# Attention projections as fill of a delta rule's stage: query, key and value products in pieces of two token tiles

## The chip, the core and the metric

The kernel runs on one core of a Trainium2 chip. Five engines work side by side, each on its own list of instructions in the order in which the program gives them: TensorE (PE) multiplies matrices, VectorE (DVE) and ScalarE (ACT) work on rows of SBUF and PSUM, GpSimd (POOL) on SBUF, and SyncE (SP) issues most transfers between the core's memory and the main memory (DMA); ScalarE issues the weights' transfers of the middle stage. Products land in PSUM and are taken out by VectorE or ScalarE. The metric is the time of one execution in microseconds (us); several executions give a median.

## What is computed

One layer of a hybrid block over 1,024 latent tokens and 256 context tokens, 1,024 channels, all in fp32. Cut to what matters:

```python
h  = rms_norm(x) * (1 + scale) + shift           # hc: the same for ctx
qkv_a, z_a, a_raw, b_raw, q_b, k_b, v_b, z_b, gates = split_cols(h @ w_in)
...
# branch A: 8 heads; q, k, v after a short convolution and SiLU, q and k normed
for d in range(2):                               # both directions
    s_ctx, _ = gdn_chunk_scan(ctx, state=0)      # chunked gated delta rule
    _, ol = gdn_chunk_scan(latent, state=s_ctx)  # o_t = S_t^T q_t
    o_lat = o_lat + ol
# branch B: differential softmax attention, 8 heads of 2 x 64
q_l = axial_rope(rms_norm(q_b, q_norm_w))
k_l = axial_rope(rms_norm(k_b, k_norm_w));  k_c = rms_norm(k_bc, k_norm_w)
o_b = (softmax(q1 k1) - lam * softmax(q2 k2)) @ v_b
merged = sig(g_a) * ((norm(o_a) * silu(z_a)) @ w_oa) + sig(g_b) * ((norm(o_b) * silu(z_b)) @ w_ob)
x = x + gate * (merged @ w_out)
```

## The kernel before

A product of fp32 precision is made of three products in the fast format: every operand is split into a high part (`hi`, a cast on ScalarE) and the rest (`lo`, a subtraction on GpSimd or VectorE), and hi x hi, hi x lo and lo x hi are summed in PSUM. So one tile of a projection is 8 x 3 = 24 products. A unit of weights is 256 columns of `w_in` in the first stages and 128 in the middle one.

The stages, as `run` (from L670) builds them:

1. The front (`front`, L239): modulation and norm of x, transposed into the tiles `hs`; among its end the first value unit, which brings the raw gates of the delta rule as well (`v_unit(0)`).
2. Eight units of queries and keys (`qk_unit`, `qk_finish`, from L591) and one of values. A unit makes ten tiles (keys) or eight (queries) of 128 tokens by 256 columns on TensorE (L456). When all are there, `qk_finish` works on the whole unit at once: square and norm, the rotation with tables (`qk_tables`), 128x128 transposes (L642), a split into two parts (L646, L647), one store for each four token tiles (L648).
3. The delta rule's projections with their convolution: one query unit (`emit_q_first`), eight of keys and values (`emit_kv`). Then the third value unit.
4. The delta rule's stage. Here the order of all engines is written by hand: streams (generators) offer one operation each with the engine, a duration, and what it waits for; `flow` (L86) takes the operation that could start first by its own clock, with a bias for each stream, and `step` emits it. The order so found is fixed in the program; each engine keeps to it on the chip. `PEL` (L55) is an amount that the planner adds before a TensorE product uses a result of another engine. The streams:
   - `preps(0)` and `preps(1)`: the preparation of heads (`gdn_prep`, L1016), two in turn. It computes the decay (ScalarE), key products `gram` and query-key products `qk` (masked on GpSimd in `masked`), stores blocks through the memory tensor `da` into `ab`, solves 31 rows of a triangular system by 62 small VectorE operations (L1089, L1091, "substitution"), brings the result back through `db`, merges blocks (`pz`, `p2`, `p3`, `pz6`, `pu6`) and stores `xd` and `qkd`.
   - `scan(0)` and `scan(1)`: the two directions' recurrences, ten chunks for each head, with products `chain` (from L1231); `out_chunk` for the outputs. Both directions of one head run side by side, the heads one after the other.
   - `loads`, `sets`, `tails`: what a scan reads, and the gated, transposed result of a head (`oT`).
   - The fill, which TensorE takes when nothing else is ready: the last value unit (`v_flow`), then 38 units of 128 columns (`fill_flow`): six query units of the delta rule (`query_out`, `query_conv`, with the convolution on VectorE) and 32 units for the gates z_a, z_b and the merge gates (`gate_out`). Their weights come by `weights`. The stage ends when the last head's tail is done; what is left of the fill is taken in the attention's opening by `rest`.
5. The attention (`attention`, a written table of due times) with the first half of the merge (`branch_a`) beside it, and the end (`phase3`).

The scans' tiles (pool `g4`, opened by `gdn_more`) lie where the last value unit's tiles and the 256-column weights lay, so scans can only start when that unit is through. SP issues in order, and so does every engine.

## Time and profile before

| | us |
|---|---|
| median of 3 runs (2168.3 to 2170.21) | 2168.44 |
| the profiled execution | 2174.7 |
| its span, first to last instruction | 2172.9 |
| mean granted clock of TensorE | 0.969 |
| busy: TensorE, VectorE, ScalarE, GpSimd | 2051.0, 1480.2, 1003.2, 938.1 |

The profile is of one execution and gives each instruction's start and length. A line number is that of the program above; `L71` is the helper through which the middle and last stages record every matrix product, so these are told apart by the names of their tiles (`mm`: projections, `chain`: scans, `s`: attention). An fp32 product outside the fast format shows as two instructions. A TensorE instruction's length is longer than its distance from the next one, since they are pipelined; a price is better read from a stretch and its count. The granted clock is the share of full speed at which TensorE was allowed to run.

### The profile page before, as it was taken

How to read it: one execution, taken by the hardware profiler on the slowest of the kernel's cores; microseconds unless marked ns; L12 is line 12 of the kernel's file. 1: busy time of each engine (PE TensorE's matmuls, PEld its weight loads, DVE VectorE, ACT ScalarE, POOL GpSimd, SP SyncE). 2: the span in 40 equal slices, each digit the busy share in tenths (PEclk: the TensorE clock that was granted, in tenths of full speed). 3: DMA queues.
4: the chain of work that ended last, by engine and by line, in shares of the span. 5: the costliest groups of instructions: out<-in, count | busy, mean ns of one | idle time of the engine just before them, and what ended most of it. 6: DMA issues, size and time to landing. Idle time of an engine off the chain costs nothing. (4 is left out here: it accounts for less than half of the span.)

```text
span 2172.9 us, 37989 instructions
## 1 busy us (share of the span) xinstructions
PE 2051.0 (94%) x14207; PEld 1719.1 (79%) x14207; DVE 1480.2 (68%) x3412; ACT 1003.2 (46%) x2133; POOL 938.1 (43%) x669
## 2 busy tenths in 40 slices
PE   8999999999999898999899899999999999998999
PEld 4999998887798677777777688776777777777899
DVE  4867776877766879788658756126788888873532
ACT  4322222443444344536545364346777777763210
POOL 2265663043322345252342424324766666764122
PEclk9999999999899899999999899998999999998999
DMA  9323335666676454565754646738454564227442
GB/s 317 97 80 127 108 107 175 164 165 171 179 180 223 122 165 148 181 210 162 235 169 154 211 152 204 210 120 230 104 149 129 148 193 130 91 83 232 144 150 86
DMA packets 379850, 347.99 MB, mean 160 GB/s; under 512 B 143007, under 2 KB 320769, under 8 KB 378643
## 3 DMA queue, kind: packets, MB, share of 16 engines
q1 hardware_dynamic: 333411, 302.05, 46.6%
q10 hardware_dynamic: 46256, 43.52, 6.2%
q8 instruction: 112, 1.84, 0.4%
q14 instruction: 71, 0.58, 0.1%
HBM read 228.96 MB, written 116.55 MB: 159 GB/s over the span
## 5 line engine op out<-in xcount | busy, mean ns | idle before, releaser
L71 PE MATMUL mm<-hs,wh 128*128 128x512 f32 x1216 | 421.5, 418 | 2.0 <-ACT zo L910 1.8
L456 PE MATMUL mm<-wh,hs 128*128 128x256 f32 (+1 forms) x1632 | 304.2, 287 | 0.5 <-DVE abt L658 0.3
L1441 DVE TENSOR_SCALAR_CACHE_REDUCE S<-s 128x512 f32<-128x512 f32 (+1 forms) x384 | 223.3, 597 | 98.4 <-PE s L71 97.2
L71 PEld LDWEIGHTS mm<-hs,wh 128*128 128x128 f32 x1216 | 234.6, 196 | 44.7 <-ACT zo L910 2.4
L456 PEld LDWEIGHTS mm<-wh,hs 128*128 128x128 f32 x1632 | 257.2, 192 | 1.1 <-DVE abt L658 0.6
L71 PE MATMUL mm<-hs,wl 128*128 128x512 f32 x608 | 253.7, 417 | 0.8 <-POOL wl L836 0.8
L433 PE MATMUL mm<-hs,wh 128*128 128x512 f32 (+1 forms) x832 | 230.9, 365 | 13.9 <-ACT xc L473 13.9
L1471 POOL TENSOR_TENSOR S<-S 128x1280 f32<-128x1280 f32 x64 | 188.5, 2945 | 109.0 <-ACT S L1466 104.2
L456 PE MATMUL mm<-wl,hs 128*128 128x256 f32 (+1 forms) x816 | 232.5, 286 | 0.0
L836 POOL TENSOR_TENSOR wl<-wr,wh 128x512 fp32r<-128x512 f32 x74 | 105.2, 1442 | 241.1 <-ACT wh L835 170.3
L433 PEld LDWEIGHTS mm<-hs,wh 128*128 128x128 f32 x832 | 151.8, 195 | 39.9 <-ACT xc L473 16.5
L1452 ACT ACTIVATE S<-S,mn 128x1280 f32<-128x1280 f32 x128 | 175.0, 1367 | 18.0 <-DVE mn L1445 17.4
L456 PEld LDWEIGHTS mm<-wl,hs 128*128 128x128 f32 x816 | 156.9, 192 | 0.0
L433 PE MATMUL mm<-hs,wl 128*128 128x512 f32 (+1 forms) x416 | 150.9, 363 | 0.0
L1487 ACT CAST ah<-t 128x512 fp32r<-128x512 f32 (+1 forms) x192 | 98.2, 512 | 101.4 <-PE t L74 98.7
L71 PE MATMUL s<-kh,qs 128*128 128x512 f32 (+1 forms) x384 | 139.5, 403 | 2.6 <-DVE S L1441 2.4
L71 PEld LDWEIGHTS mm<-hs,wl 128*128 128x128 f32 x608 | 119.5, 197 | 22.3 <-POOL wl L836 1.3
L478 DVE SCALAR_TENSOR_TENSOR ac<-xc,smallT,ac 128x1284 f32<-128x1284 f32 (+1 forms) x72 | 122.8, 1705 | 10.5 <-ACT ac L474 8.6
L1089 DVE TENSOR_TENSOR tmp<-ab,ts 80x31 f32<-80x31 f32 (+15 forms) x248 | 116.6, 470 | 16.3 <-DMA ab<-da 10.4
L1091 DVE TENSOR_TENSOR ts<-ts,tmp 80x31 f32<-80x31 f32 (+15 forms) x248 | 121.7, 491 | 6.1
L1494 DVE TENSOR_TENSOR al<-t,ah 128x512 fp32r<-128x512 f32 (+1 forms) x192 | 113.6, 592 | 7.7 <-ACT ah L1487 7.3
L74 PE MATMUL t<-ct,S 128*128 128x128 f32 x640 | 103.4, 277 | 6.8 <-DVE al L1494 6.8
(312 smaller groups left out, 5053.8 us busy)
## 6 DMA issues: line engine op xcount, KB each, us to landing
wr<-in_w_in_dram SPq DMA_DIRECT2D x21, 1024.0 KB
wr<-in_w_in_dram ACTq DMA_DIRECT2D x37, 512.0 KB
X<-gcd SPq DMA_DIRECT2D x16, 640.0 KB
xd<-X SPq DMA_DIRECT2D x16, 640.0 KB
x<-xd SPq DMA_DIRECT2D x80, 128.0 KB
kh<-kd SPq DMA_DIRECT2D x32, 320.0 KB
wa<-in_w_ada_dram SPq DMA_DIRECT2D x8, 1024.0 KB
qd<-col SPq DMA_DIRECT2D x16, 512.0 KB
```

Of the source, the lines that this page charges most:

```text
L71: self.nc.tensor.matmul(out, lhsT, rhs, start=start, stop=stop)
L74: self.nc.tensor.transpose(out, src, self.ident[:src.shape[0], :src.shape[0]])
L433: nc.tensor.matmul(pt[:, :n], wt[:, k, cs], ht[:, k, o:o + n], start=i == 0, stop=i == 3 * KT - 1)
L456: nc.tensor.matmul(pt[:, j * W:j * W + n], ht[:, k, ts], wt[:, k, :n], start=i == 0, stop=i == 3 * KT - 1)
L478: nc.vector.scalar_tensor_tensor(ac[:, w], xc[:, o + j:o + j + wd // parts], self.convw(j, ct), ac[:, w], ALU.mult, ALU.add)
L836: t2 = yield POOL, 1.36, [t1], lambda: nc.gpsimd.tensor_tensor(lo[:, k], raw[:, k], hi[:, k].bitcast(F32), ALU.subtract)
L1089: t = yield DVE, n * w / 960.0 + 0.11, [t, t1], lambda: V.tensor_tensor(tv, ab[:, j + 1:, j:j + 1].to_broadcast([80, n, w]), ts[:, j, :w]. ...
L1091: t = yield DVE, n * w / 960.0 + 0.11, [t, t1], lambda: V.tensor_tensor(ts[:, j + 1:, :w], ts[:, j + 1:, :w], tv, ALU.subtract)
L1441: self.nc.vector.tensor_scalar(x[c][:, o:o + m], x["s", j, c][:, :m], 1.0, None, ALU.mult, ALU.min, accum_out=x["m3"][:, c, j:j + 1])
L1452: self.nc.scalar.activation(S, S, AF.Exp, bias=x["mn"][:, c:c + 1], scale=-1.0, accum_out=w["l0"][:, c, t:t + 1])
L1471: self.nc.gpsimd.tensor_tensor(x[0], x[0], x[1], ALU.add)
L1494: self.nc.vector.tensor_tensor(y["al", k][:, :, q], x["t", k][:, :nb * P].rearrange("p (j f) -> p j f", f=P), y["ah", k][:, :, q].bitcast( ...
```

## The change

The delta rule's projections come right after the first value unit: all four query units (`emit_q`), then as before keys and values between them, and one value unit. The attention's eight query and key units and two of three value units become "parts", the first fill of the delta rule's stage, in the order keys, values, queries. A part's tile is now finished by itself, two token tiles (128 x 512) at a time in two slots: three ScalarE operations take it out of PSUM (`part_out`), then norm, rotation, transposes, split and two stores of 128 KB or so follow (`part_post`). Then come 32 gate units as fill; the six query units and their convolution are no longer in the stage.

```diff
-PEL = 0.05
+PEL = 0.4
...
+    def load_w(self, src, ab=False):
...
         for s in range(2):
             k = slice(s * KT // 2, (s + 1) * KT // 2)
-            nc.scalar.copy(hi[:, k], raw[:, k])
+            raw = self.wr.tile([P, KT // 2, n], F32, tag="wr", name="wr")
+            nc.sync.dma_start(raw[:, :, :w], src.rearrange("(k p) n -> p k n", p=P)[:, k])
...
+            nc.scalar.copy(hi[:, k], raw)
...
-                        self.units(qk + vs[:1], kv[0])
+                kv = qu[:1] + [... keys and values as before ...] + qu[1:]
...
+                parts = [("k", p) for p in range(4)] + [("v", 2), ("v", 3)] + [("q", p) for p in range(4)]
...
+                    def fill():
+                        yield from self.part_flow(parts)
+                        self.zo = self.hc.tile([P, 2, L], F32, tag="s21", name="zo")
+                        yield from self.fill_flow(todo)
+
+                    def more():
+                        yield lambda: sum(self.posted) == sum((NL if k == "q" else NT) // 2 for k, _ in parts)
+                        cx.close()
+                        self.gdn_more(gr)
+                        yield lambda: False
...
-                        self.flow(lambda: self.tailed == H)
+                    self.flow(lambda: self.tailed == H and self.units_done >= len(todo) - self.LEFT)
...
+    def part_flow(self, parts):
...
+            for t0 in range(0, NL if kind == "q" else NT, 2):
+                yield lambda: len(free) > self.nb
+                pt = self.pm.tile([P, 512], F32, tag="mm", name="mm")
+                for j in range(2):
...
+                            t = yield PE, 0.1195, [free[self.nb], tw], lambda: self.mm(
+                                pt[:, j * W:j * W + W], ht[:, k, o:o + P], wt[:, k], m == 0, m == 3 * KT - 1)
...
+    def part_out(self, kind, pair, t0, pt, t, free, n):
+        nc, s, tk = self.nc, n % 2, self.tk
+        yield lambda: self.posted[s] >= n // 2
...
+        for hf in range(2):
+            tr = yield ACT, 0.35, [t, old], lambda: nc.scalar.copy(raw[:, hf]...., v[:, hf])
+        t = yield ACT, 0.478, [t, old], lambda: nc.scalar.activation(sq, pt, AF.Square)
...
+    def part_post(self, kind, pair, t0, raw, sq, tr, t, s):
...
+        t = yield DVE, 0.6, [t], lambda: V.tensor_reduce(ss, ...)
+        tw = yield DVE, 0.08, [t], lambda: V.tensor_scalar(ss, ss, 1.0 / 64, EPS, ALU.mult, ALU.add)
...
+            for hf in range(2):
+                t1 = yield POOL, 0.7, [t, tr, tt], lambda: Q.tensor_tensor(m[hf], x[1 - hf], T(1, 1 - hf), ALU.mult)
+                if hf == 0:
+                    tw = yield POOL, 1.65, [tw], lambda: self.power(ss, ss)
+                t2 = yield DVE, 0.35, [tr, tt], lambda: V.tensor_tensor(o[hf], x[hf], T(0, hf), ALU.mult)
+                te += [(yield DVE, 0.35, [t1, t2], lambda: V.tensor_tensor(o[hf], o[hf], m[hf], ...))]
...
+        te = yield POOL, 1.3, [te, tw], lambda: Q.tensor_tensor(f8, f8, ss..., ALU.mult)
...
+                t1 = yield PE, 0.109, [te, b], lambda: self.tr(...)
...
+        th = yield ACT, 0.478, [t1, self.slot_t[s]], lambda: nc.scalar.copy(col[0], pv)
+        tl = yield DVE, 0.6, [th, self.slot_t[s]], lambda: V.tensor_tensor(col[1], pv, col[0].bitcast(F32), ALU.subtract)
...
-        self.asides[0].append(self.masked(h, qk, tQ))
+        self.kT_t, self.gram = [tX[1][-1], tQ], h + 1
...
+                    if n == "qk":
+                        u["tqk"] = yield POOL, 0.72, [u["tqk"]], lambda: nc.gpsimd.tensor_tensor(
+                            x, x, (self.up, self.lo)[d].unsqueeze(1).to_broadcast([P, 2, P]), ALU.mult)
...
+    LEFT = 3
-    FB0 = 0.2
+    FB0 = 0.0
-    BIAS = (0,0,0,0,0)
+    BIAS = (0, 0, -0.3, 0, 0)
```

Dots inside a line stand for shortened arguments. Besides:

- The mask of the query-key products moves from the preparation (two GpSimd operations a head on 128x1024) to `loads` (eight a head on 128x256), and `qkd` is stored in four pieces a head instead of one.
- Weights of the first stages come as two halves through two buffers of half the size (`load_w`); part weights by `part_weights`, half of each split on GpSimd and half on VectorE, with their transfers on ScalarE's queue.
- The rotation's table for the queries is stored to memory (`tbd`) and read back when the queries' parts begin.
- Preparations wait for no query unit any more; the second head's tiles (`g3`) exist from the start. `oa` lies with the scans' tiles and `oT` with the attention's.
- The stage now ends when the last tail is done and at most three gate units (`LEFT`) are left. The planner's biases are -0.3 for taking pieces out and finishing them, and 0 instead of 0.2 for fill.

More of the change, by code (lines that the diff above doesn't have):

```diff
@@ L696, in run @@
                         self.pm = self.spool(cp, "pm", 4, space=PSUM)
[L697 to L699 removed]
+                        self.units([self.v_unit(0, before)], kv[0])
                     with ExitStack() as st:
@@ L745, in run @@
-                    with tc.manual_schedule(engines={E.PE}):
-                        gr.close()
-                        self.att_pools(zr)
-                        self.filler = self.rest()
-                        att = self.attention()
-                        next(att)
-                        for _ in self.filler:
-                            pass
+                self.tk = self.spool(cx, "tk2")
+                self.filled = {}
+                first, head = self.gdn_first(gr, zr)
+                self.qk_tables()
@@ L753, in run @@
+                with tc.manual_schedule(engines={E.PE}):
+                    gr.close()
+                    self.att_pools(zr)
+                    self.filler = self.rest()
+                    att = self.attention()
+                    next(att)
+                    for _ in self.filler:
+                        pass
             left.close()
@@ new lines, with part_cols, part_weights @@
+    NPART = 10
+    @staticmethod
+    def part_cols(kind, pair):
+        return {"q": C_QB, "k": C_KB, "v": C_VB}[kind] + pair * W
+    def part_weights(self, parts):
+        raw = lambda s: (self.wr.tile([P, KT // 2, W], F32, tag="wr", name="wr"), self.raw_t[s])
+        for i, p in enumerate(parts):
+            if i:
+                yield lambda: self.parts_done >= i - 1
+                yield from self.weight(raw, *(self.wab[i % 2].tile([P, KT, W], F32R, tag=n, name=n) for n in ("wh", "wl")),
+                                       self.part_cols(*p), W, [self.part_t.get(i - 2)], self.parts_, i, (POOL, DVE))
@@ L885, in v_flow @@
                             m += 1
[L886 to L899 removed]
+                self.evacs.append(self.part_out(kind, pair, t0, pt, t, free, self.nb))
@@ L1012, in preps @@
         for h in range(s, H, 2):
-            yield lambda: self.gh[s] and C_Q + h * P in self.filled and self.stored > h - 2
+            yield lambda: self.stored > h - 2
             yield from self.gdn_prep(h)
```

418 lines of the change are left out of this document (168 added, 250 removed).

## The prediction

> **What bounds the kernel now.** I read the page first, then the busy time of each stage, then the waits of TensorE, then single operations.
>
> ```profile
> span 2172.9 us, 37989 instructions
> PE 2051.0 (94%) x14207; PEld 1719.1 (79%) x14207; DVE 1480.2 (68%) x3412; ACT 1003.2 (46%) x2133; POOL 938.1 (43%) x669
> ```
>
> TensorE is busy for 94% of the span, and the chain of waits ends on it. The change removes no product: the two programs order the same 12,098 matrix products and transposes. So it can gain only time that TensorE now loses. Where it loses time is read by stage (columns: stretch, length, then busy time of TensorE, weight loads, VectorE, ScalarE and GpSimd, granted clock, DMA share, GB/s):
>
> ```profile
> 93.00:350.00 257.00, 247.61 (x2056) 246.09 (x2055) 191.11 (x234) 59.59 (x132) 145.65 (x48) 0.99 0.33 110
> 350.00:620.00 270.00, 256.12 (x1282) 216.91 (x1281) 197.97 (x258) 117.37 (x271) 72.30 (x91) 0.97 0.63 168
> 620.00:655.00 35.00, 35.00 (x293) 34.93 (x292) 19.42 (x18) 12.28 (x24) 7.04 (x4) 1.00 0.86 223
> 655.00:795.00 140.00, 125.93 (x881) 103.63 (x879) 111.08 (x256) 57.43 (x108) 49.55 (x44) 0.93 0.54 171
> 795.00:890.00 95.00, 83.83 (x693) 69.75 (x694) 79.34 (x190) 49.37 (x128) 40.19 (x40) 0.93 0.56 176
> 890.00:984.00 94.00, 88.17 (x716) 73.62 (x714) 75.52 (x177) 44.85 (x124) 34.22 (x36) 0.94 0.58 186
> 984.00:1062.00 78.00, 75.43 (x672) 63.26 (x673) 64.94 (x171) 40.75 (x110) 30.75 (x33) 1.00 0.63 200
> 1062.00:1156.00 94.00, 83.46 (x675) 69.24 (x674) 50.63 (x138) 51.50 (x135) 33.35 (x36) 0.93 0.60 188
> 1156.00:1257.00 101.00, 87.04 (x715) 72.78 (x715) 75.17 (x189) 48.43 (x128) 38.71 (x39) 0.93 0.57 174
> 1257.00:1319.00 62.00, 62.00 (x612) 53.22 (x611) 32.85 (x100) 35.28 (x101) 26.89 (x31) 1.00 0.56 176
> 1319.00:1417.00 98.00, 91.03 (x738) 75.46 (x736) 43.45 (x132) 37.82 (x105) 34.96 (x38) 1.00 0.62 195
> 1417.00:1475.00 58.00, 57.25 (x329) 49.87 (x330) 16.73 (x55) 24.03 (x77) 14.78 (x16) 0.95 0.36 116
> 1475.00:1520.00 45.00, 43.12 (x182) 26.24 (x181) 32.75 (x119) 31.09 (x49) 25.38 (x11) 0.77 0.82 228
> ...
> 1000.00:1050.00 50.00, 48.61 (x492) 41.36 (x493) 46.19 (x116) 23.50 (x77) 26.65 (x30) 1.00 0.52 172
> ...
> 1395.00:1410.00 15.00, 15.00 (x67) 12.42 (x67) 0.00 (x0) 1.79 (x3) 2.02 (x2) 1.00 0.80 200
> ```
>
> First and last starts of the delta rule's first product, of a head's first scan product and of the gate products (columns: shortest, median and longest in ns, first and last start), the longest waits of TensorE in this stage (total, times, longest), and two products one chunk apart in the last head's scan:
>
> ```profile
> L71 PEld LDWEIGHTS gram<-kT x160: 186/192/193, 655.4 to 1300.5; 128*128 128x128 f32 x160
> ...
> L71 PE MATMUL chain<-vv,x x32: 270/304/583, 795.2 to 1419.4; 128*128 128x128 f32 x32
> ...
> L71 PE MATMUL mm<-hs,wh x1216: 387/389/795, 684.8 to 1474.5; 128*128 128x512 f32 x174
> ...
> PE pu L71 <- DVE Z L1151: 12.2, 5, 4.4
> PE pq L71 <- DVE qss L954: 10.2, 3, 4.3
> PE chain L71 <- DMA x<-xd: 9.2, 4, 4.2
> ...
> 1427.76 0.42 PE L71 MATMUL chain<-S,sk 128*128 128x128 f32 x2
> ...
> 1430.98 0.42 PE L71 MATMUL chain<-S,sk 128*128 128x128 f32 x2
> ```
>
> The attention's queries and keys, with a quarter of the values, run from 93 to 350 at 247.6 of 257 us busy and clock 0.99. The delta rule starts at 655.4 and its scans at 795.2; one head follows the other. From 655 to 1417 the clock is 0.93 in four of eight stretches, TensorE idles for 10 to 14 us in the same four, and it waits for VectorE's and ScalarE's results, for the last query convolutions (pq) and for a prepared head that has just been stored (x<-xd). Fill itself never ran short: the last gate products start at 1474.5. In 1395 to 1410, where nothing but fill ran, 67 products of 512 columns took 15.0 us, 0.225 us each; the unit from 620 to 655 gives 35.0/293 = 0.1195 us for one of 256 columns. A scan product is 0.22 us. In these prices the work ordered before the first scan (338 products of 512 columns, 183 of 256, 14 us of preparation) is 112 us of 140, and that from 795 to 1475 (1,486 x 0.225, 812 x 0.22, 50 us of small products) 563 us of 680: 0.80 and 0.83 of the time. The scans alone could go faster: in the last head one chunk follows another after 1430.98 - 1427.76 = 3.22 us, so ten chunks take 32 us, while a head takes 60 to 100.
>
> **The change, before the scans start.** The stage from 93 to 350 goes, except for one value unit (240 products, 29 us), and so does the value unit at 620. Three query units come in front: 288 products at 0.225 make 65 us, at the 0.92 of the stretch from 350 to 620 (256.1 busy at clock 0.97) 71 us. The first 93 us and the 270 us of key and value convolutions stay: 93 + 270 + 71 + 29 = 463 us to the delta rule's first product, 192 earlier. Of these 192, 186 us are work that now lies in the delta rule's stage; 6 are lost time saved. Weights come in halves through two buffers; the cast of a unit still runs during the unit before it, so I cost that at nothing (a DMA that came late would cost a few us a unit).
>
> In the order of the changed program, 2,149 products of 256 columns (257 us), 96 gate products (22 us), 144 transposes (16 us) and four heads' preparation (36 us) stand on TensorE between the first key product and the first scan: 331 us. No scan can start earlier, because its tiles take the place of the piece tiles. TensorE is not what sets this window. The rows for the other engines, from groups of operations (busy time, mean ns), single tiles (shortest, median, longest) and the stretch of the present rotation (start and length in us):
>
> ```profile
> L1091 DVE TENSOR_TENSOR ts<-ts,tmp 80x31 f32<-80x31 f32 (+15 forms) x248 | 121.7, 491 | 6.1
> L1089 DVE TENSOR_TENSOR tmp<-ab,ts 80x31 f32<-80x31 f32 (+15 forms) x248 | 116.6, 470 | 16.3 <-DMA ab<-da 10.4
> ...
> L1089 DVE TENSOR_TENSOR tmp<-ab,ts x248: 170/372/2862, 684.3 to 1358.1; 80x31 f32<-80x31 f32 x8, 80x87 f32<-80x87 f32 x8, 80x135 f32<-80x135 f32 x8, 80x175 f32<-80x175 f32 x8
> ...
> L1064 DVE SCALAR_TENSOR_TENSOR X<-gram,beta,X 128x128 f32<-128x128 f32 x160 | 49.4, 344 | 2.4 <-PE gram L71 0.9
> ...
> L954 DVE TENSOR_REDUCE qss<-xq 128x16 f32<-128x512 f32 x12 | 8.1, 678 | 0.7 <-ACT xq L953 0.7
> ...
> L647 DVE TENSOR_TENSOR col<-tr,col 128x512 fp32r<-128x512 f32 (+1 forms) x40 | 24.3, 633 | 28.7 <-ACT col L646 28.7
> ...
> L394 DVE TENSOR_TENSOR wl<-wr,wh 128x1024 fp32r<-128x1024 f32 (+1 forms) x21 | 44.4, 2116 | 24.8 <-ACT wh L393 24.8
> ...
> 125.84 2.92 DVE L626 TENSOR_TENSOR fin<-raw,tbq 128x1024 f32<-128x1024 f32 x1 [2.10 <-POOL raw L618]
> 128.68 3.42 DVE L629 TENSOR_TENSOR fin<-raw,tbq 128x1024 f32<-128x1024 f32 x1
> 135.37 1.21 DVE L628 TENSOR_TENSOR fin<-fin,m 128x1024 f32<-128x1024 f32 x1
> ...
> 127.64 3.39 POOL L630 TENSOR_TENSOR m<-raw,tbq 128x1024 f32<-128x1024 f32 x1
> ...
> L634 DVE TENSOR_TENSOR fin<-raw,gk x8: 410/1517/2625, 160.0 to 346.1; 128x256 f32<-128x256 f32 x8
> ...
> L1544 POOL TENSOR_TENSOR oT<-oT,sz 128x256 f32<-128x256 f32 x32 | 22.8, 735 | 0.0
> ...
> L836 POOL TENSOR_TENSOR wl<-wr,wh 128x512 fp32r<-128x512 f32 x74 | 105.2, 1442 | 241.1 <-ACT wh L835 170.3
> ...
> L181 POOL TENSOR_TENSOR of<-of,mhalf x8: 1637/1656/1737, 849.1 to 1459.1; 128x8 f32<-128x8 f32 x8
> ```
>
> Four heads' substitution is 248 operations at 0.48 us, 119; their other steps, 88 at 0.344 among them, about 80. Each of 36 pieces adds a sum of squares (0.68), a small scaling (0.16) and a split (0.63): 53 us. Eight halves of a weight split at 2.1 are 17, ten value splits 7. New is the rotation in pieces of 128x256, 124 operations with both inputs in SBUF. The row of 135.37 shows such an operation four times as wide, alone, at 1.21; those at 125.84 and 128.68 took 2.92 and 3.42 because each ended only after the GpSimd product beside it. So one piece costs at least 0.41 (the shortest of the row fin<-raw,gk, which has this width) and at most 0.41 x 3.42/1.21 = 1.15. I take 0.65, nearer to the lower: a GpSimd product of this width takes 0.74, and the substitution, which meets GpSimd's products too, averages 0.470 over a median of 0.372. That is 84 us with the ctx pieces, 360 in all. GpSimd gets 36 x (1.66 + 1.44) + 64 x 0.74 = 159 us more and stays near 240 of 410. ScalarE's two copies, square and cast of a piece lie beside this. SP, which issues in order, gets 92 stores of pieces and 24 more of query-key products; one that waits for its split holds up the preparation's stores and loads behind it, and a transpose that waits on TensorE holds up the next piece's products. Both wait for VectorE, so its time holds them too, and I add nothing. The rotation table's way through memory (once), the moved tiles of oa and oT and the planner's FB0 and BIAS change no engine's work; they go at nothing within the bounds below.
>
> By parts of the window, from the two engines' orders: keys and queries need 282 us of VectorE and 234 of TensorE; at the 0.92 of VectorE's best stretch (46.2 of 50, from 1000 to 1050) that is 307 us. The values between them need 75 of TensorE and 63 of VectorE, 79 us; the ends are 24. Together 410 us; the scans start at 873. Bounds: with everything on VectorE hidden, 331/0.95 = 348 us (0.95 is 247.6 x 0.99/257); with 1.15 a rotation, 124 x 0.5/0.92 = 67 more, 477.
>
> **Scans to the end.** By then four heads are stored and a fifth substituted, and only three substitutions fall into the scans (VectorE 342 us in all). TensorE's work from the first scan to the last head's output transposes is 1,108 x 0.225 + 772 x 0.22 + 35 = 454 us, some 57 a head, above the 32 that a scan needs. The waits for x and pq go; those for Z stay for half of the heads, and the planner now allows 0.35 us more before a product that uses another engine's result (PEL). Of the stretches above, those with clock 1.00 were busy for 228 of 238 us, 0.96, against 0.89 for all of 795 to 1475 (busy times clock); 0.83 x 0.96/0.89 = 0.90 is the upper bound, 0.83 the lower. I take 0.89, near the upper because most of these waits lose their place: 510 us. The mask of the query-key products is now 64 small GpSimd operations in place of 16; 46 us against 38, hidden under 510. Then come 224 gate products alone, 51 us. The attention and the end took 2172.9 - 1475 = 698 us; 108 gate products (24 us) are moved into the attention's opening, where TensorE lost 1.9 idle and 43.1 x 0.23 = 10 us to the clock; I count 10 as filled again: 712.
>
> Sum: 463 + 410 + 510 + 51 + 712 = 2146 us against 2172.9, 27 less. The profiled execution took 2174.7 in all, 6.3 above the median of the runs; so 2168.4 - 27 = 2141.
>
> **Rivals.** *A, slower: the port.* In 124 to 137 us VectorE's two-input operations and GpSimd's products took turns. If every rotation in pieces meets one, it costs 1.15, the window is 477 and the time 2208. It decides from a mean of 0.85 on, where the 27 us are used up (27 x 0.92/124 = 0.2). For it: the pieces put the two engines' products of one piece side by side. Against: the product beside it is only 0.74 us long, so that a piece which meets it waits less than that. The Trainium skill, "SBUF — State Buffer", section "Who interferes with whom", says that a VectorE instruction with two SBUF inputs and a GpSimd instruction that reads SBUF share one port pair, and that the later one fully blocks. By that rule this rival is the outcome whenever the two meet; the rows at 125.84 and 128.68 agree, and what no row shows is how often the pieces meet.
>
> *B, faster: VectorE is hidden.* Nothing then takes up the idle time but TensorE: the window is 348, the time 2141 - 62 = 2079. For it: the value parts and the late gate products are pure fill, and the rotations may run in GpSimd's pauses. Against: 282 us of VectorE beside 234 of TensorE.
>
> *C, slower: the lost share stays.* The change fills a stage that never lacked fill, so scans keep 0.83: 547 us, 37 more, 2178. For it: work is moved from a stage that loses 5% into one that loses 17%. Against: the waits for x and pq have no place any more.
>
> That the scans become the bound is out: 32 us of latency lie under 57 of work.
>
> **How the numbers follow.** Forecast 0.43, A 0.19, B 0.22, C 0.16. The measurement tells about 0.2% (4.3 us) from no change. B and 0.41 of the forecast are faster: 0.63. A and 0.11 of C are slower: 0.30. The rest of C and of the forecast, 0.07, lies between. The forecast's own range is 2115 to 2165; the whole reaches from B's 2079 to just short of A's 2208, 2205.
>
> **What would show it.** Right: the first key product near 463, the first scan near 873, VectorE over 0.85 busy between them in the key and query parts and TensorE with gaps there; about 64 us from one head to the next; rotations averaging 0.65. Wrong: rotations near 1.1 or a window over 450 (A); a window near 350 (B); heads at 70 us with clock 0.93 (C). A start later than 480 would say that the convolutions lost more in front than I allow.

## The result and the profile after

| | before | after |
|---|---|---|
| median, 20 runs each in turn on one chip (us) | 2166.26 (2153.57 to 2172.29) | 2177.37 (2166.09 to 2189.89) |
| ratio, 95% interval | | 1.0058 [1.0041, 1.0076] |
| the profiled execution (us) | 2174.7 | 2166.09 |
| its span and mean granted clock | 2172.9, 0.969 | 2164.3, 0.979 |

The changed kernel is 0.6% slower, 11 us, where 27 us less were forecast. The two profiled executions say the opposite, 8.6 us faster, and this must be cleared first: the profiled execution of before is longer than all of its 20 runs, that of after is the shortest of its 20. A hundredth of clock would be 22 of 2,170 us if TensorE set the time throughout; over the 20 runs of the changed kernel the time falls by about 17 us with each hundredth, loosely (correlation -0.7). So single spans of these two can't be subtracted; the first experiment repeats both.

The page of the changed kernel, as quoted of before:

```profile
span 2164.3 us, 38617 instructions
PE 2021.1 (93%) x14207; PEld 1704.9 (79%) x14207; DVE 1431.2 (66%) x3438; ACT 1021.4 (47%) x2154; POOL 964.3 (45%) x804
```

TensorE has the same 14,207 instructions and is idle for 143 us instead of 122 (span less busy time). By stage (columns as in the prediction: stretch, length, busy TensorE, weight loads, VectorE, ScalarE, GpSimd, clock, DMA share, GB/s), and the window's inner part:

```profile
93.00:363.00 270.00, 251.52 (x1263) 212.59 (x1262) 213.08 (x288) 115.37 (x270) 76.72 (x83) 0.97 0.60 157
363.00:465.00 102.00, 94.28 (x526) 82.61 (x526) 78.50 (x85) 47.30 (x67) 16.18 (x19) 0.97 0.50 145
465.00:480.00 15.00, 8.33 (x67) 8.16 (x66) 8.27 (x16) 8.76 (x19) 6.25 (x5) 0.92 0.57 187
480.00:866.00 386.00, 350.56 (x3600) 336.75 (x3598) 313.44 (x694) 141.84 (x303) 208.58 (x194) 0.96 0.53 159
866.00:1393.50 527.50, 496.63 (x3897) 423.08 (x3898) 297.63 (x866) 263.47 (x767) 229.36 (x270) 0.98 0.61 187
1393.50:1447.50 54.00, 51.56 (x227) 42.02 (x226) 0.75 (x1) 12.25 (x22) 14.17 (x11) 1.00 0.77 202
1447.50:2164.00 716.50, 687.67 (x4149) 542.30 (x4147) 464.46 (x1361) 393.22 (x644) 389.14 (x196) 0.99 0.46 136
...
560.00:640.00 80.00, 71.92 (x783) 69.11 (x781) 73.44 (x153) 24.64 (x51) 49.94 (x49) 0.96 0.42 120
640.00:720.00 80.00, 74.04 (x836) 72.32 (x837) 52.25 (x119) 31.08 (x71) 22.52 (x24) 0.96 0.69 216
720.00:800.00 80.00, 71.92 (x782) 70.43 (x781) 72.80 (x164) 27.69 (x61) 53.50 (x49) 0.96 0.44 126
```

The stages are all where the forecast put them: the convolutions end at 465, the pieces run until the first scan product at 866, the scans until 1393, then gate products alone, then 717 us of attention and end. VectorE is 0.92 busy in the stretch of keys and 0.91 in that of queries, and 0.65 in the values between them. The first starts and the rotation's lengths, by tile:

```profile
L71 PE MATMUL gram<-kq x288: 270/275/550, 479.3 to 1136.9; 128*128 128x128 f32 x144
...
L71 PE MATMUL chain<-vv,x x32: 270/275/580, 866.1 to 1328.4; 128*128 128x128 f32 x32
...
L895 DVE TENSOR_TENSOR fin<-fin,sq x64: 383/425/2595, 476.0 to 846.0; 128x256 f32<-128x256 f32 x64
L903 POOL TENSOR_TENSOR fin<-fin,ss x36: 1037/1044/1276, 479.6 to 846.5; 128x512 f32<-128x512 f32 x36
L894 DVE TENSOR_TENSOR fin<-raw,tb x32: 407/415/974, 474.9 to 620.4; 128x256 f32<-128x256 f32 x32
```

TensorE's longest waits, by stretch (363 to 482, the window, the scans and what follows them):

```profile
PE pq L484 <- DVE qss L482: 7.7, 1, 7.7
PE gram L71 <- issue: 6.7, 1, 6.7
...
PE tr L74 <- POOL fin L903: 19.2, 17, 3.3
...
PE chain L71 <- DMA vv<-gv: 5.8, 3, 3.0
...
PE chain L71 <- DMA sz<-sza: 3.9, 1, 3.9
...
PE chain L71 <- DMA x<-xd: 3.1, 2, 2.3
```

Two single waits stand in front that the forecast does not have. The page names nothing for the second ("issue"); the timeline around it does (columns: start, length, then the instruction, and the engine's idle time before it):

```profile
472.42 0.58 ACT L588 CAST vt<-mm 128x512 fp32r<-128x512 f32 x1 [4.59 <-DMA vd<-vt]
...
474.86 0.73 POOL L891 TENSOR_TENSOR sq<-raw,tb 128x256 f32<-128x256 f32 x1 [5.78 <-DVE ss L881]
474.89 0.97 DVE L894 TENSOR_TENSOR fin<-raw,tb 128x256 f32<-128x256 f32 x1
...
478.48 0.68 DVE L589 TENSOR_TENSOR vt<-mm,vt 128x512 fp32r<-128x512 f32 x1
...
479.26 2.04 PE L71 MATMUL gram<-kq 128*128 128x128 f32 x8 [6.67 <-issue]
```

The value unit ahead of the stage is taken out of PSUM through one buffer (`vt` in `v_out`), so each piece waits for the store of the one before (4.59 us). The first key product starts 0.10 us after such an evacuation has ended (478.48 + 0.68 = 479.16), as it would if it waited for that bank of PSUM; `after_v1two` below tests this.

### The profile page after: what moved, and what is told of

It reads as the page before. It is cut to its first block, busy times and chain, and to the rows that moved or that the text cites. A ratio compares the mean times of both kernels' runs of the same rounds, so it can differ in the third digit from the quotient of the medians.

```text
span 2164.3 us, 38617 instructions
## 1 busy us (share of the span) xinstructions
PE 2021.1 (93%) x14207; PEld 1704.9 (79%) x14207; DVE 1431.2 (66%) x3438; ACT 1021.4 (47%) x2154; POOL 964.3 (45%) x804
## 5 line engine op out<-in xcount | busy, mean ns | idle before, releaser
L71 PE MATMUL mm<-hs,wh 128*128 128x512 f32 x1024 | 362.6, 415 | 2.4 <-ACT zo L932 2.4
L423 PE MATMUL mm<-hs,wh 128*128 128x512 f32 (+1 forms) x1024 | 290.8, 370 | 18.0 <-ACT xc L463 18.0
L71 PE MATMUL mm<-wh,hs 128*128 128x256 f32 x1472 | 280.9, 290 | 0.0
L71 PEld LDWEIGHTS mm<-wh,hs 128*128 128x128 f32 x1472 | 237.3, 197 | 0.9
L71 PE MATMUL mm<-wl,hs 128*128 128x256 f32 x736 | 214.0, 291 | 0.0
L71 PE MATMUL mm<-hs,wl 128*128 128x512 f32 x512 | 211.8, 414 | 0.0
L423 PE MATMUL mm<-hs,wl 128*128 128x512 f32 (+1 forms) x512 | 188.4, 368 | 0.0
L468 DVE SCALAR_TENSOR_TENSOR ac<-xc,smallT,ac 128x1284 f32<-128x1284 f32 (+1 forms) x96 | 157.9, 1645 | 9.1 <-ACT ac L464 6.8
L780 POOL TENSOR_TENSOR wl<-hx,wh 128x512 fp32r<-128x512 f32 x64 | 83.9, 1311 | 140.3 <-ACT wh L779 111.7
L423 PEld LDWEIGHTS mm<-hs,wl 128*128 128x128 f32 x512 | 99.0, 193 | 15.3
```

What stands on the lines that cost most here:

```text
L71: self.nc.tensor.matmul(out, lhsT, rhs, start=start, stop=stop)
L423: nc.tensor.matmul(pt[:, :n], wt[:, k, cs], ht[:, k, o:o + n], start=i == 0, stop=i == 3 * KT - 1)
L468: nc.vector.scalar_tensor_tensor(ac[:, w], xc[:, o + j:o + j + wd // parts], self.convw(j, ct), ac[:, w], ALU.mult, ALU.add)
L780: t2 = yield e, (1.42 if e == POOL else 0.63) * w / P, [t1], lambda: (nc.gpsimd if e == POOL else nc.vector).tensor_tensor(lo[:, k], r, hi ...
```

## The experiments

Each kernel was run beside the kernel before on one chip; the ratio is to that. "Idle" is the span less TensorE's busy time, from the kernel's page; "clock" is that of its profiled execution.

**Both kernels again.** No edit.

> The kernel before, unchanged, for its granted clock in ordinary executions. Theory 1 (the profiles were an unlike pair): before was profiled at clock 0.969 (2174.7 us) and the changed kernel at 0.979 (2166.1), while the changed kernel's 20 runs go from 2166 at 0.979 to 2185 at 0.970, about 2.1 us for a thousandth; then before's ordinary runs of 2166 have a clock of 0.972 to 0.975, and at equal clock the changed kernel is 9 to 14 us slower. Theory 2 (the change itself costs clock): before's ordinary runs have 0.978 or more, against the changed kernel's 0.9745.

> The changed kernel, unchanged, for a second profile at an ordinary clock (0.973 to 0.976). Both theories: 1.004 to 1.008 of before. Theory 1: the stages' idle times repeat within 3 us each and only the throttled stretches move. Theory 2: more throttled stretches in the window between 465 and 866 us than the kernel before has in its stage from 93 to 350.

Before: 2166.08 us, 1.0007 [0.9991, 1.0022], profiled at clock 0.972, span 2167.6. After: 2176.54, 1.0049 [1.0032, 1.0067], at 0.975, span 2180.9. Before's twelve runs have a median clock of 0.973. Theory 1 holds: at ordinary clocks the changed kernel is slower in the profiles too, and it is not slower because of the clock. Only its idle times do not repeat as well as it says: from the first scan product to the attention they are 33 us in one profile of the changed kernel and 39 in the other. The stages of before, repeated:

```profile
0.00:93.00 93.00, 83.38 (x528) 60.47 (x529) 58.00 (x137) 39.42 (x64) 23.14 (x20) 1.00 0.71 230
93.00:651.00 558.00, 535.20 (x3625) 495.21 (x3623) 409.75 (x509) 190.26 (x429) 222.86 (x143) 0.99 0.51 147
651.00:788.00 137.00, 122.09 (x879) 101.66 (x878) 110.45 (x256) 56.29 (x104) 48.06 (x44) 0.96 0.55 172
788.00:1473.00 685.00, 630.30 (x5141) 528.28 (x5142) 438.28 (x1150) 332.74 (x905) 253.76 (x268) 0.96 0.56 178
1473.00:2167.50 694.50, 672.67 (x4040) 526.98 (x4038) 463.77 (x1361) 385.34 (x634) 386.63 (x194) 0.97 0.49 143
```

and those of the changed kernel, repeated:

```profile
0.00:93.00 93.00, 80.50 (x491) 57.32 (x492) 55.02 (x128) 39.25 (x64) 23.96 (x27) 1.00 0.68 221
93.00:482.50 389.50, 354.78 (x1849) 302.97 (x1847) 294.93 (x388) 171.57 (x356) 99.83 (x106) 0.96 0.56 154
482.50:867.50 385.00, 350.62 (x3601) 336.66 (x3601) 313.82 (x696) 141.94 (x303) 209.00 (x194) 0.97 0.53 160
867.50:1457.50 590.00, 550.79 (x4120) 467.38 (x4121) 298.86 (x867) 275.75 (x787) 243.29 (x281) 0.98 0.61 186
1457.50:2181.00 723.50, 695.86 (x4150) 549.06 (x4148) 464.35 (x1361) 393.89 (x644) 389.73 (x196) 0.98 0.45 134
```

Length less busy time gives TensorE's idle time. Up to the first key product: 9.6 + 22.8 = 32 us before, 12.5 + 34.7 = 47 after. Delta rule's stage: 14.9 + 54.7 = 70, and 34.4 + 39.2 = 74. Attention and end: 22 and 28. Together 124 and 148. The clock takes 2167.6 x 0.028 = 61 and 2180.9 x 0.025 = 55 us. What is left, 1983 and 1978 us, is TensorE at work. So the whole difference of 13 us between these two spans is 24 us more waiting, less 6 of clock and 5 of work. Some 15 of the 24 lie in front, 4 in the stage and 6 behind it; the 4 is within what two profiles of one kernel differ by.

**The value unit's buffers** (`after_v1two`):

```diff
-        tags = ("ch0", "cl0") if pair else ("vh", "vl")
+        i = t0 // 2 % 2
+        tags = (f"ch{i}", f"cl{i}") if pair else ("vh", "vl")
```

> The evacuation of the one value unit that stands ahead of the delta rule's stage gets two buffers in place of one. Theory (a wait that I had not priced): its five pieces wait for their stores, 4 to 5 us each, so the first key product gets its PSUM bank at 479.2, 6.7 us after the last product before it; with two buffers the gap goes and the whole is 6 to 7 us faster than the changed kernel (0.997 of it, near 1.002 of before). Rival (the delta rule is bound by VectorE in this stretch anyway): the first scan product stays near 866 and the time within 2 us of the changed kernel.

2173.09 us, 1.0027 [1.0010, 1.0044]. The gap is gone and the first key product is 7.5 us earlier than in the repeated profile:

```profile
L71 PE MATMUL gram<-kq x288: 270/275/542, 475.1 to 1143.6; 128*128 128x128 f32 x144
```

So it was the buffer. The first scan product comes 4.5 us earlier (863.0), and 3.4 us arrive at the end, which lies between theory and rival; the intervals overlap, so the size is not sure. With the new lengths below, the same edit went from 2133.35 to 2129.68.

**The query columns' small product** (`after_pqlate`): `pq` and what uses it become a function that the next call of `emit_q` runs.

> The small product of a query column's sum of squares is issued one column later, behind the next column's products. Theory: the wait of 6.3 to 7.7 us at 391 to 399 us goes, last product of the front at 461 in place of 467.9, 5 to 7 us faster than the changed kernel. Rival (VectorE and ScalarE are behind here anyway, and TensorE waits for its next PSUM bank instead): last product of the front not before 466, time within 2 us.

2179.81 us, 1.0071 [1.0052, 1.0090]. The wait stayed (7.5 us, pq on qss): the order of engines in this part is not that of the program's calls, and the product still starts right behind its own column's sum (397.5, the sum started at 396.2). The edit did not do what was meant, so what the wait costs is not shown.

**The gates in the attention's opening** (`after_left0`): `LEFT = 3` becomes 0.

> LEFT goes from 3 to 0: no gate unit is left for the attention's opening. Theory (the moved gate products fill nothing there: net TensorE time of the part from the first score product on rose from 654 to 680 us by these 24 us, and idle from 22 to 28): the same time as the changed kernel within 3 us, that part back near 695, the products alone near 80. Rival (10 of the 24 us are hidden in the opening, as I had forecast): 8 to 12 us slower than the changed kernel, ratio to before near 1.010.

2180.06 us, 1.0077 [1.0058, 1.0096]. No more than 3.5 us, but the test is weak: only the first five score products moved ahead of the gate products, which still ran alone, 56.39 us busy of 58. What speaks on the forecast's point are the last lines of the two repeated profiles: the attention's part is 29 us longer with 108 gate products of 24 us in it, and in `after_costs` below, where none are left for it, it takes 699.5 us, near before's 694.5. They fill nothing.

**The planner's constant** (`after_pel05`): `PEL = 0.4` becomes 0.05.

> The planner's constant PEL goes back from 0.4 to 0.05. Theory (0.4 helps): TensorE waits more often for results of other engines, idle time from the first key product to 1447 us grows from 69 to 80 or more, 5 to 15 us slower than the changed kernel. Rival (0.4 puts scans off and costs): 3 us or more faster, heads under 65 us apart.

2176.57 us, 1.0048 [1.0030, 1.0065]: no difference from 2176.54, so both expected times fell. The last scan starts at 1285 instead of 1334, so the rival's second part is right, but the products left for the end of the stage take 108 us instead of 56. Here it only moves fill.

**Without the rotation** (`after_norot`): every piece goes the way of the ctx pieces, so queries and keys are not rotated.

```diff
-        if t0 < NL:
+        if t0 < 0:
```

> Leaves out the rotation: each piece's halves are only scaled (two VectorE operations in place of four, no GpSimd product), so queries and keys are not rotated. Theory (VectorE bounds the window's key and query parts): 64 operations of 0.45 us less on VectorE and 47 us less on GpSimd shorten the stretch from the first key product to the first scan product from 386 to 360 or less, idle from 35 to about 20; 15 to 25 us faster than the changed kernel. Rival (only TensorE's own work counts, 336 us of it): the stretch stays above 375.

2157.57 us, 0.9970 [0.9959, 0.9982], 19 us under the changed kernel:

```profile
479.50:847.00 367.50, 344.17 (x3668) 332.18 (x3668) 301.28 (x707) 137.79 (x302) 162.83 (x141) 0.98 0.57 174
```

The window is 17 us shorter with 23 us idle, between the theory's 360 and the rival's 375. So VectorE bounds the window at most in part. The edit also takes 46 us off GpSimd (208.6 to 162.8 busy) and gives the planner a new order; what either does of the 17 us is not separated.

**Measured lengths in the planner** (`after_costs`, and its two halves `after_sub` and `after_piece`). The planner had 0.11 us + n*w/960 for each substitution operation, 0.29 on average, and 0.35 for the rotation's. In the changed kernel's window they take, by groups (busy time and mean ns, idle time before them):

```profile
L1065 DVE TENSOR_TENSOR ts<-ts,tmp 80x31 f32<-80x31 f32 (+15 forms) x124 | 68.1, 550 | 2.1
L1063 DVE TENSOR_TENSOR tmp<-ab,ts 80x31 f32<-80x31 f32 (+15 forms) x124 | 63.4, 511 | 6.4 <-DMA ab<-da 4.3
L895 DVE TENSOR_TENSOR fin<-fin,sq 128x256 f32<-128x256 f32 x63 | 29.6, 471 | 11.2 <-POOL sq L891 7.9
...
L894 DVE TENSOR_TENSOR fin<-raw,hx 128x256 f32<-128x256 f32 x32 | 13.7, 429 | 0.0
```

The edit changes no engine's work, only the written order.

```diff
-            t = yield DVE, n * w / 960.0 + 0.11, [t, t1], ...
+            t = yield DVE, n * w / 960.0 + 0.31, [t, t1], ...
...
-                t2 = yield DVE, 0.35, [tr, tt], ...
+                t2 = yield DVE, 0.43, [tr, tt], ...
-                te += [(yield DVE, 0.35, [t1, t2], ...
+                te += [(yield DVE, 0.47, [t1, t2], ...
-        t = yield DVE, 0.6, [t], lambda: V.tensor_reduce(...
+        t = yield DVE, 0.68, [t], lambda: V.tensor_reduce(...
```

(The small scaling goes from 0.08 to 0.2 and the power from 1.65 to 1.94; the substitution's second operation is changed like the first.)

> The planner is given the measured lengths of VectorE's substitution (0.20 us more each), rotation, sums and of the power on GpSimd. Theory (TensorE waits because the written order rests on too short lengths): idle from the first key product to 1457 us falls from 73 to 55 or less, 10 us or more faster than the changed kernel, level with before. Rival (VectorE's amount of work sets it, not the order): within 4 us of the changed kernel.

> Of the planner's new lengths only the substitution's (0.20 us more for each of its operations). Theory (the substitution is what the planner had wrong: 496 operations at a planned mean of 0.29 us that take 0.48 to 0.53): it holds 30 us or more of the 44 that all new lengths gained, 2135 to 2147, and only three of eight substitutions stand ahead of the first scan product. Rival (the pieces' lengths did it): 2165 or more.

> Of the planner's new lengths only the pieces' (rotation, sum, small scaling, power). Theory (substitution): within 10 us of the changed kernel, 2167 to 2180, four substitutions ahead of the first scan product. Rival: 2150 or less.

All lengths: 2133.35 us, 0.9854 [0.9836, 0.9873], 43 us faster than the changed kernel and 1.5% faster than before. The substitution's alone: 2160.34, 0.9982 [0.9965, 1.0000]. The pieces' alone: 2196.42, 1.0154 [1.0128, 1.0179], 20 slower. The effects don't add: -16 and +20 make -43. All lengths, by stage:

```profile
479.00:835.00 356.00, 341.57 (x3299) 329.52 (x3299) 265.38 (x592) 129.46 (x270) 200.25 (x181) 0.97 0.52 157
835.00:1435.50 600.50, 575.98 (x4531) 487.96 (x4531) 343.98 (x970) 297.44 (x829) 253.45 (x295) 0.98 0.60 186
1435.50:2135.00 699.50, 672.85 (x4041) 525.79 (x4039) 463.68 (x1362) 385.72 (x635) 387.78 (x195) 0.97 0.49 145
```

Idle time is 14 us in the window and 25 in the scans against 34 and 39, and no gate product is left for the opening. In the window VectorE now does 93 of the 248 operations of the substitution's first kind, three heads, instead of 124, four:

```profile
L1063 DVE TENSOR_TENSOR tmp<-ab,ts 80x31 f32<-80x31 f32 (+15 forms) x93 | 48.3, 519 | 1.1
```

**One head's substitution later, with the old lengths** (`after_late4`):

```diff
-        yield lambda: self.subst == h
+        yield lambda: self.subst == h and (h < 3 or self.gs is not None)
```

> The planner's old lengths, but the fourth head's substitution may not begin before the last piece is out and the scans' tiles exist. Theory 1 (a place: one substitution of some 55 us too many lies in the window, where VectorE is full, instead of beside the scans, where it is 40% idle): the window falls from 385 to 365 or less, idle from 34 to 25 or less, and the whole is 10 to 25 us faster than the changed kernel. Theory 2 (the fine order of pieces, products and substitution, which follows from all lengths together): within 5 us of the changed kernel, since the lengths stay as they were.

2183.11 us, 1.0081 [1.0056, 1.0107]. The window fell by 9 us, from 385 to 376, and the stretch from the first scan product to the last output transposes rose from 534 to 562. That one head's place explains the gain falls.

**Right lengths, or a lucky order?** Half (`after_costs_half`), nine tenths (`after_costs_09`), eleven tenths (`after_costs_11`) and one and a half times (`after_costs_more`) of what the new lengths add.

> Half of what the measured lengths add (0.10 us for a substitution operation, the pieces' likewise). Theory 2 with the lengths as its cause: between the changed kernel and all lengths, 2140 to 2165. Rival (each change of a length draws a new order, good or bad by chance): outside of 2133 to 2177, or equal to one end.

> Nine tenths of what the measured lengths add (0.18 us for a substitution operation, the pieces' likewise). Theory 2 (right lengths lead to a good order, and half or one and a half are too far off): within 12 us of the 2133 of the full lengths. Rival (every change draws a new order by chance): more than 20 us from it, as the draws so far, 2133 to 2196, are spread.

> Eleven tenths of what the measured lengths add (0.22 us for a substitution operation, the pieces' likewise). Theory 2: within 12 us of the 2133 of the full lengths. Rival (chance): more than 20 us from it.

> One and a half times what the measured lengths add (0.30 us for a substitution operation, the pieces' likewise). Theory 2 with the lengths as its cause: the right lengths are the best, so 2133 to 2155. Rival (chance): above 2165, or below 2125.

2180.86, 2159.64, 2153.55 and 2177.37 us, against 2133.35 in the middle. The two near ones lie 26 and 20 us off: chance has most of it. They still lie 17 and 23 us under the changed kernel, half and one and a half times do not. So lengths near the measured ones may help by some 20 us; the rest of 2133 is a good draw. More than that these runs don't settle.

**The kernel before with longer substitution lengths** (`before_sub`: 0.20 us more, `before_sub10`: 0.10 us more).

> The kernel before, with the substitution's measured length (0.20 us more) in its planner. Theory (the wrong lengths hurt mainly the changed kernel, because there four heads' substitution share VectorE with the pieces while TensorE has no scans to go on with): 0 to 15 us faster than before. Rival (the old order loses as much by it): 25 us or more faster than before, and then the moved projections themselves are no gain even with right lengths.

> The kernel before with half of the substitution's added length (0.10 us). Theory (in the old order the scans wait for the head just prepared, and a longer planned substitution is stretched further, so x comes later): between 2170 and 2205, waits of the scans for x above 9 us. Rival (chance): 2160 or less.

2211.79 us, 1.0221 [1.0195, 1.0247], and 2192.01, 1.0130 [1.0110, 1.0151]. Neither theory of the first had this: the old order gets worse, and with the larger step more. With 0.20 us more its scans wait for the stored head, 33.8 us in place of 9.2:

```profile
PE chain L71 <- DMA x<-xd: 33.8, 4, 28.4
```

One of these waits is 28.4 us. In the order of before a scan needs the head that has just been prepared, so a preparation that is stretched holds it up. With 0.10 us more the time is within what was expected, but the wait for x is 8.6 us, not longer than before; there the products that wait for `oa` (18.6 us) and `vd` (17.1) lost it:

```profile
PE oT L74 <- POOL oa L1330: 18.6, 4, 8.7
PE chain L71 <- ACT vd L1262: 17.1, 6, 5.5
PE chain L71 <- DMA x<-xd: 8.6, 5, 3.2
```

So the late head is shown for the one order and not for the other. What they have in common is one wait ahead of the scans that before does not have, for the first head's merge product `pz` (first `before_sub`, then `before_sub10`):

```profile
734.73 1.41 PE L71 MATMUL pz<-RR,X 32*32 32x32 f32 x80 [16.47 <-issue]
...
731.92 1.29 PE L71 MATMUL pz<-RR,X 32*32 32x32 f32 x71 [11.71 <-issue]
```

In both it starts right after VectorE has transposed `RR` (L1099), and that operation stands behind steps of a query's convolution (L941), of which one takes 5.8 and 5.2 us where the median is 0.74. In the two orders 16 of the 41 and 12 of the 18 us of added idle time are this wait.

**Both gains** (`after_costs_v1two`): all new lengths and the two buffers.

> All new lengths, and two buffers for the evacuation of the value unit ahead of the stage. Theory (its gap of 7 us and the lengths are separate losses): 3 to 7 us faster than the new lengths alone, 2126 to 2130, 0.982 of before. Rival (VectorE takes the time back in the window): within 2 us of them.

2129.68 us, 0.9840 [0.9814, 0.9866], the fastest of all.

All versions that compute the same, in order of idle time:

| version | median us | idle us | clock |
|---|---|---|---|
| after_costs_v1two | 2129.7 | 105 | 0.977 |
| after_costs | 2133.4 | 110 | 0.976 |
| before_again | 2166.1 | 124 | 0.972 |
| after_costs_11 | 2153.6 | 127 | 0.979 |
| after_sub | 2160.3 | 130 | 0.975 |
| after_costs_09 | 2159.6 | 131 | 0.973 |
| after_costs_more | 2177.4 | 136 | 0.968 |
| after_left0, after_pqlate | 2180.1, 2179.8 | 138 | 0.975, 0.976 |
| before_sub10 | 2192.0 | 142 | 0.965 |
| after_late4 | 2183.1 | 147 | 0.970 |
| after_v1two, after_again | 2173.1, 2176.5 | 148 | 0.975 |
| after_pel05 | 2176.6 | 152 | 0.976 |
| after_costs_half | 2180.9 | 153 | 0.975 |
| after_piece | 2196.4 | 158 | 0.969 |
| before_sub | 2211.8 | 165 | 0.963 |

Span less idle time less clock loss is 1960 to 1983 us in all of them.

## Why the prediction was wrong, by its steps

- *The convolutions in front, 463 us.* They ended at 465. The first key product came at 479 to 483, since 7 us of the first part's products stand ahead of it, and then the wait for the value unit's buffer. TensorE idles 15 us more in front. Two waits that I had not priced, 6 to 8 us each, that one and `pq`, are 14 of it; the waits for a bank that ScalarE empties in the convolutions rose from 12.5 to 20.1 us, and 9 of waiting for the old rotation's transposes went. My step "6 are lost time saved" had the sign wrong: the stage from 93 to 350 goes with its 9 us, but in its new place TensorE waits 19.2 us for the pieces (`tr` on `fin` above).
- *The window, 410 us.* 385 to 387. VectorE was as busy as I said (0.92 and 0.91 in keys and queries, gaps in TensorE before the transposes), but the rotation averaged 0.43 to 0.47 us, not 0.65. This term was too long by 24, while the substitution was 12 longer (131.5 us). The lengths of all of VectorE's operations there add up to 346 us in 313 of busy time, since one starts before the other has ended; my 360 was a sum of lengths. The window made up for the late start: the first scan product came at 866, 7 us from my 873, by luck.
- *Scans, "I take 0.89, near the upper because most of these waits lose their place: 510 us".* This is the step that failed most: 527 and 534, 0.86 and 0.85 of the time for the same 454 us of work. Lost time was to be 56 us and is 73 and 80. Before, 680 - 563 = 117 us were lost: 52 of waiting, 29 of clock (0.957 from 795 to 1475), and 36 by which TensorE, at full clock, was busy for longer than my prices give. After, the first profile has 31 of waiting (527.5 - 496.63), 8 of clock (0.984) and 34; the repeated one 34.6, 11.8 (0.978) and 33.6. The last part was in the forecast: 0.83/0.89 carries it over, 454 x 0.89/0.83 = 487 us, and both profiles have 488 without waits and clock. What failed is waiting and clock: of 510 us the forecast left 23 for the two, and they took 39 and 46. The 0.96 behind it was read from the stretches whose clock was 1.00, which are also those with little waiting. The waits for x fell from 9.2 to 3.1 us as forecast, and in this stretch those for Z and pq are no more; but scan products now wait for vv and sz, which are read back from memory (5.8 and 3.9) and which they did not wait for before, and for the state S as before (4.8 and 4.7).

  Where the 34 us come from is not shown. Prices from products of one kind in a row are a suspect, because here the kinds alternate. From the starts of neighbouring instructions in the two repeated profiles (key products counted with the scans', waits included):

```
                                              before (788-1464)   after (867.5-1401.5)
product of 512 columns, next the same          1194 x 0.248 us      745 x 0.258 us
product of 512 columns, next a scan's           215 x 0.381 us      346 x 0.318 us
a scan's, next a product of 512 columns         213 x 0.040 us      331 x 0.031 us
```

  One way, a change of kind costs 0.06 to 0.13 us. On the way back the fast product starts 0.03 to 0.04 us behind the scan's instruction, where another of the scan's comes after 0.11, so most of it returns. At full clock and without waits, the way from a scan product over a run of fast ones to the next scan product is only 0.03 us longer than the prices give: 5 us in 184 such runs before and 9 in 312 after.
- *Gate products alone, 51 us.* 54 to 56.
- *Attention and end, "I count 10 as filled again: 712".* 717 and 723; nothing was filled, and TensorE idles 6 us more there.
- *The sum.* In the repeated profile, against 2146: +20, -25, +24, +5 and +11, together 35. In the first, +16, -23, +17, +3 and +5, together 18, at a clock of 0.979.
- *Rival A, the port.* Fell: the rotation's mean is far under its 0.85. Where a piece starts well inside GpSimd's product, it ends 0.28 us after that product (474.89 + 0.97 = 475.86 above, beside 474.86 + 0.73 = 475.59), so it takes 0.97 us in place of 0.41, and 2.6 at most, beside the split of a weight. That the later of the two is blocked until the other is done is the rule of the Trainium skill in "SBUF — State Buffer", "Who interferes with whom"; the trace agrees. But only 10 of the 128 rotations took more than 0.5 us. Another 14 started in the last 0.1 us of such a product and lost nothing.
- *Rival B.* Fell: no order of the changed kernel had a window under 355 us.
- *Rival C.* Its time, 2178, is the result's, but not by its signs: heads follow one another after (1328.4 - 866.1)/7 = 66 us, not 70, at clock 0.98, not 0.93. Its mechanism, that the scans keep their lost share, is half to two thirds of the way there (0.86 and 0.85, between 0.89 and 0.83). That its time came out is luck: the front and the opening were longer than it has them, the window and the scans shorter.

Behind these steps stands one that they share. I treated the share of lost time as belonging to a stage, to be carried over or dropped with its work. With the same instructions, the changed kernel took 2133 to 2196 us when only the lengths in its planner changed, and the kernel before 2166 to 2212. A gain of 27 us was less than what a new order wins or loses. The order that came out with this change lies in the middle of the eight tried by lengths alone; that of before is the best of its three. Whether a gain lies in the moved projections apart from this is not shown: the fastest version of the changed kernel is 35 us under before, but before was not searched as widely.

## What to carry to other kernels

A change that makes a planner write a new order moves the time twice, by what is moved and by the new order; rerun the planner with a few lengths varied before the change is judged, and give the forecast at least that spread. A stage's lost time should be split into waits, clock and what the prices miss before any of it is carried over. Here the last part stayed as it was, and of the waits, which the forecast dropped with their cause, others took the place. A share read from stretches chosen for their full clock leaves out both. Buffers that a change halves need a price of their own, even for a single unit.

## What the hardware showed that was not expected

In the front, a convolution step of 1.55 us took 3.74 beside GpSimd's product of 2.37 (the repeated profile of the changed kernel, 251 us):

```profile
248.22 1.55 DVE L468 SCALAR_TENSOR_TENSOR ac<-xc,smallT,ac 128x1284 f32<-128x1284 f32 x1
...
251.90 3.74 DVE L468 SCALAR_TENSOR_TENSOR ac<-xc,smallT,ac 128x1284 f32<-128x1284 f32 x1
251.92 2.37 POOL L555 TENSOR_TENSOR kb<-ac,kb 128x1024 f32<-128x1024 f32 x1
...
257.61 1.27 ACT L470 ACTIVATE ac<-ac 128x1284 f32<-128x1284 f32 x1 [12.91 <-DVE ac L468]
```

ScalarE stood behind the four steps of this column for 12.91 us, and TensorE's longest wait of that stretch, 6.2 us for a freed bank, lies there. Of the 12.91 us, 2.5 are what this step and the next (1.88) took above 1.55 each, and 2.1 are a copy of 128x10 between them that took 2.30 us beside another GpSimd product, where others take 0.17. All steps longer than 1.6 us together lost 18 us in the changed kernel's 96 and 13 us in the 72 of before. So what rival A feared for the pieces was paid in the convolutions, which stand in both kernels.

And the clock follows the waits. The profiles' record of the granted clock has two values here, full and half. In the twenty profiles a stretch at half clock begins inside or less than 0.5 us behind 109 of TensorE's 137 waits of 4 us or more (20 of the other 28 are the first wait of each execution), and at only 16 of its 1,291 waits of 0.2 to 1.5 us. The wait for x of 4.5 us that ends at 1414.2 in the repeated profile of before is one of the 109:

```profile
1412.10:1422.10 10.00, 7.44 (x25) 6.27 (x26) 1.63 (x5) 2.29 (x6) 1.58 (x3) 0.50 0.72 235
```

So a long wait is paid twice. Summed over a kernel the relation is loose: 0.963 with 165 us idle and 0.977 with 105, but 0.976 with 152 (`after_pel05`).
